# A mixture of experts in full fp32: the order of wide and narrow experts, a narrow expert 0, and ten additions taken off GpSimd

## The chip, the cores and the metric

The kernel runs on one core of one Trainium2 chip. Its time is the device time of one execution, in microseconds (us), here the median of several runs. A profile is one execution recorded instruction by instruction. TensorE, VectorE, ScalarE and GpSimd appear in it as PE (with its weight loads as PEld), DVE, ACT and POOL; SP is the queue that issues the weight loads.

## The reference

A decoder of two layers on 256 tokens of width 1024, all in float32. Layer 0 is retention and a dense SwiGLU; layer 1 is a pooling mixer and a SwiGLU with eight experts, of which each token uses two. Each part starts with an RMSNorm whose output is scaled and shifted by vectors (`mod`) worked out from a second input, and ends in a gated addition to the residual. Cut to what matters here:

```python
h = rmsnorm(x) * (1 + scale) + shift              # scale, shift from c @ ada_w + ada_b
x = x + g1 * pool_mixer(h)                        # window sums, 4 products of 256 x 256, bias, scale
h = rmsnorm(x) * (1 + scale2) + shift2
top, idx = top_k(h @ router, 2); gates = softmax(top)
for e in range(8):                                # each on the tokens that chose it
    y_e = (silu(h_e @ gate[e]) * (h_e @ up[e])) @ down[e]     # 1024 x 3584, 1024 x 3584, 3584 x 1024
x = x + g2 * (sum of a token's two y_e, times its two gates)
return rmsnorm(x)
```

## The kernel before

**Full precision from two rounded halves.** A float32 weight is too exact for TensorE's fast form, so it is taken in two parts. ScalarE writes the rounded weight (`w_hi`), VectorE the remainder (`w_lo = raw - w_hi`), both in `split`, line 109. Weights come through one queue, SP's, as pieces of 128 x 2048 (1.05 MB, "a half": half of the 128 x 4096 that one matrix of one block holds) into a ring of `raw` buffers. Of `w_hi` and `w_lo` there are `N_SPL` = 3 buffers each.

**The expert layer** is 456 to 1371 us of the span. Tokens of an expert are gathered into slots by a product with a one-hot matrix. An expert is worked on in 7 blocks of 512 hidden columns; each block has three matrices (gate, up, down), so six halves. There are 56 blocks, and the program issues for block i: gate, up, and then the down product of block i-2.

- A *wide* expert has 128 slots. Its tokens too are split in a rounded part and a remainder, and each tile takes three matmuls (`mm3`, lines 152 to 154): 24 for a matrix, 72 for a block. TensorE then transposes the product (`moe_T`) and VectorE splits it (`dT<-tbank,dT`).
- A *narrow* expert has 64 slots. Rounded part and remainder of its tokens stand side by side as 128 columns, and two matmuls a tile do the work (`mm2`, lines 731 and 732): 48 for a block. `fold_T` adds the two parts by matmuls with a folding matrix; VectorE has a product (`h_n`) and a split (`dT<-h_n,dT`), each half as long as the wide block's.

The splits of weights, six on ScalarE and six on VectorE, are the same in both kinds.

**The order.** Expert 0 is wide and comes first, while the kernel still works out which experts have more tokens: `ordering()` ranks experts 1 to 7 by their count, the first three are wide, the others narrow. `PLACES` gives the rank worked on at each place: (expert 0), 3, 0, 4, 1, 5, 2, 6. Places 0, 2, 4 and 6 are thus wide and 1, 3, 5 and 7 narrow, each as seven blocks in a row. Around block 5 of an expert `prepare` issues the next one's one-hot matrix, its gather in two or four steps and a transpose; the steps are spread over blocks by `step()`. After an expert's last down product `combine` scales its sum (`take`, VectorE, two halves) and adds it to the residual (`give`, four products). If some expert had more tokens than slots (`room`), a repair pass at the end would work on all experts again.

What sets the order on an engine is the order in which the program issues; what is issued inside `behind(...)` is put after the middle split of the next matrix on its engine. Each engine works through its own list in order and waits on semaphores.

**GpSimd** has 14 instructions. Eight add a column to a column of `mod` in the first stage (line 271, one in each of eight rounds in which VectorE makes two sums for `mod`), two add a 128 x 1024 row to the residual in the pooling mixer (line 505).

Of the kernel before, what the change touches and what calls it, by code (L numbers as in the profile page):

```python
# [10 lines left out]
F = mybir.dt.float32  # L11
# [8 lines left out]
P = 128  # L20
# [25 lines left out]
N_RAW, N_SPL, N_E8 = 6, 3, 4  # L46
# [4 lines left out]
PLACES = (None, 3, 0, 4, 1, 5, 2, 6)  # L51
WIDE = tuple(r is None or r < N_WIDE for r in PLACES)
# [8 lines left out]
def trunk(ctx, tc, x, cols, c_row, const, ada_0, ada, w_0, w_in, w_out, f_gu, f_dn, pool_w, m_g, m_u, m_d, out):  # L61
# [46 lines left out]
    def split(hi, lo, src, engine=nc.vector):  # L108
        return nc.scalar.activation(hi, src, AF.Copy), engine.tensor_sub(lo, src, hi.bitcast(F))  # L109
# [159 lines left out]
    for k in range(KD):  # L269
        ada_sums(ada_0[k], (k, 8 + k), None if k else ada_first)  # L270
        nc.gpsimd.tensor_add(mod[:, k:k + 1], mod[:, k:k + 1], col[:, C_ADAB + k:C_ADAB + k + 1])
# [276 lines left out]
    for b in range(TB):  # L548
# [4 lines left out]
        lT = act.tile([NE, P], F, tag="ohT", name="lT", bufs=2)  # L553
# [12 lines left out]
    above = small([TB, NE, 2, NE], "above")  # L566
# [11 lines left out]
    def sources():  # L578

        def rows(a, i):  # L580
            p, j = divmod(i, NJ)
            if p == 0:
                return a[j * P:(j + 1) * P, :]
            if expert[p] is None:
                expert[p] = nc.values_load(place_i[0:1, PLACES[p]:PLACES[p] + 1], engines=[SP], min_val=1, max_val=NE - 1,
# [50 lines left out]
    def ordering():  # L636
# [9 lines left out]
        over = small([N, 2, N], "over")  # L646
# [6 lines left out]
        at = small([N, N], "at")  # L653
        nc.vector.tensor_tensor(at, rank.rearrange("p (o e) -> p o e", o=1).to_broadcast([P, N, N]),
                                iota[:, 0:N].rearrange("p (r o) -> p r o", o=1).to_broadcast([P, N, N]), op=ALU.is_equal)
        part = small([N, N], "part")
# [17 lines left out]
        nc.vector.memset(room[:, 0:1], float(P))  # L674
# [23 lines left out]
    def prepare(slots, sels, narrow=False, quick=False):  # L698


        oh = one_hot(slots, sels, narrow)
        xe = buf("a8", [KD, 2, HALF] if narrow else [2, KD, P], 2, R, name="xe")
        ohT = buf("ohT", [T], 2, R)
# [3 lines left out]
        def gather(n):  # L707
            ps = tbank()
# [76 lines left out]
    def combine(ye, ohT, gates, g2_row, last=False):  # L785
# [37 lines left out]
    steps = []  # L823

    def step():
        if steps:
            steps.pop(0)()

    def turned_of(i, parts):
        return fold_T(parts) if WIDE[i // NJ] is False else moe_T(parts)  # L830

    def picked(a, placed, p):
        return pick(a, 0) if p == 0 else pick(placed, PLACES[p])

    outs, ths = {}, {}

    def down_of(i):
        p, j = divmod(i, NJ)
# [3 lines left out]
        if j == NJ - 1 and p < NE - 1:  # L842
# [159 lines left out]
```

## Time and profile before

| | |
|---|---|
| time, median of 3 runs | 1397.23 us (1395.9 to 1397.43) |
| the profiled execution: its own time | 1396.38 us |
| its span (first to last instruction) | 1394.1 us |
| granted TensorE clock, mean | 0.994 |
| busy: TensorE, VectorE, ScalarE, GpSimd | 96%, 87%, 70%, 1% |
| weights read | 475 MB, 342 GB/s over the span |

The busy share counts the time in which at least one instruction of the engine was under way. A listed matmul lasts longer than the step from one to the next, since matmuls overlap; their rate is read from starts. A row's "idle before" is the time for which its engine stood still ahead of it, and the name behind `<-` is what ended that.

### The profile page before, as it was taken

To read this page: it belongs to the slowest core of one execution; us is meant where nothing else is said; L and a number is where in the kernel's file an instruction comes from. 1 tells how busy PE (TensorE), PEld (TensorE's weight loads), DVE (VectorE), ACT (ScalarE), POOL (GpSimd) and SP (SyncE) were. 2 spreads that over 40 slices of the span, in tenths; PEclk is the share of its full clock that TensorE was granted. 3 is DMA by queue.
4 is the path that set the end of the run, shared out by engine and by line. 5 is a ranking of instruction groups with operands and counts; after the bars stand their busy time and mean duration, and the time that the engine had idled before them with its cause. 6 is when DMAs were issued, how large, how long until landed. Compare 5 with 4: busy or idle time off the path is not lost.

```text
span 1394.1 us, 16978 instructions
## 1 busy us (share of the span) xinstructions
PE 1336.6 (96%) x6220; PEld 1075.7 (77%) x6220; DVE 1217.7 (87%) x1120; ACT 972.5 (70%) x921; POOL 14.2 (1%) x14
## 2 busy tenths in 40 slices
PE   7999999999998999999999999999999999999996
PEld 5788876888886888877788777878877778887774
DVE  7889867988857898899999799899879989979997
ACT  6555465433435777888877788887778888768885
POOL 1100000000001000000000000000000000000000
PEclk9999999999999999999999999999999999999998
DMA  9977885998786699899999899999989999998980
GB/s 383 373 265 261 323 293 193 356 380 348 272 354 247 252 381 346 314 393 414 393 400 359 329 393 359 421 374 372 379 319 401 398 393 400 358 376 334 386 369 33
DMA packets 66475, 477.32 MB, mean 342 GB/s; under 512 B 7377, under 2 KB 7761, under 8 KB 8658
## 3 DMA queue, kind: packets, MB, share of 16 engines
q1 hardware_dynamic: 66386, 476.17, 88.2%
q8 instruction: 51, 0.84, 0.2%
q14 instruction: 38, 0.31, 0.1%
HBM read 475.10 MB, written 1.05 MB: 342 GB/s over the span
## 4 chain that ended last, share of the span: by engine, by line
PE 67%; DVE 16%; DMA 8%; ACT 4%; issue 4%; SPq 0%; DVEq 0%; ACTq 0%
PE bank L153 18%; PE bank L154 18%; PE bank L152 18%; DVE w_lo L109 13%; DMA raw<-in_m_g_dram 4%; ACT w_hi L109 3%; PE bank L732 3%; PE bank L731 3%; DMA raw<-in_m_u_dram 2%; PE tbank L713 2%; PE tbank L246 1%; PE tbank L767 1%; DMA raw<-in_m_d_dram 1%; DVE xs L804 1%; ACT xe_f L236 1%
## 5 line engine op out<-in xcount | busy, mean ns | idle before, releaser
L109 DVE TENSOR_TENSOR w_lo<-raw,w_hi 128x2048 fp32r<-128x2048 f32 (+1 forms) x413 | 911.9, 2228 | 109.8 <-ACT w_hi L109 108.4
L109 ACT ACTIVATE w_hi<-raw 128x2048 fp32r<-128x2048 f32 (+1 forms) x413 | 765.1, 1866 | 234.1 <-PE bank L154 193.7
L732 PE MATMUL bank<-w_lo,xe 128*128 128x512 f32 x448 | 183.6, 410 | 15.1 <-DVE w_lo L109 11.6
L153 PE MATMUL bank<-w_lo,xe 128*128 128x512 f32 x448 | 176.7, 395 | 6.6 <-DVE w_lo L109 6.2
L731 PE MATMUL bank<-w_hi,xe 128*128 128x512 f32 x448 | 175.7, 393 | 1.4 <-ACT w_hi L109 1.4
L152 PE MATMUL bank<-w_hi,xe 128*128 128x512 f32 x448 | 176.0, 393 | 0.3 <-ACT xe L109 0.3
L154 PE MATMUL bank<-w_hi,xe 128*128 128x512 f32 x448 | 174.6, 390 | 0.0
L152 PE MATMUL bank<-w_hi,T_h 128*128 128x512 f32 x352 | 141.9, 403 | 3.0 <-ACT T_h L109 3.0
L153 PE MATMUL bank<-w_lo,T_h 128*128 128x512 f32 x352 | 140.1, 398 | 2.4 <-DVE w_lo L109 2.4
L154 PE MATMUL bank<-w_hi,T_l 128*128 128x512 f32 x352 | 140.1, 398 | 0.5 <-DVE T_l L109 0.4
L732 PEld LDWEIGHTS bank<-w_lo,xe 128*128 128x128 f32 x448 | 84.1, 188 | 57.4 <-DVE w_lo L109 41.7
L153 PE MATMUL bank<-w_lo,dT 128*128 128x512 f32 x312 | 123.3, 395 | 0.9 <-DVE w_lo L109 0.9
L154 PE MATMUL bank<-w_hi,dT 128*128 128x512 f32 x312 | 121.8, 390 | 0.0
L152 PE MATMUL bank<-w_hi,dT 128*128 128x512 f32 x312 | 114.5, 390 | 0.0
L163 DVE SCALAR_TENSOR_TENSOR raw<-raw,cb 128x1024 f32<-128x1024 f32 x96 | 114.3, 1217 | 0.3 <-DMA raw<-in_ada_dram 0.3
L153 PEld LDWEIGHTS bank<-w_lo,xe 128*128 128x128 f32 x448 | 84.2, 188 | 26.2 <-DVE w_lo L109 9.5
L152 PEld LDWEIGHTS bank<-w_hi,xe 128*128 128x128 f32 x448 | 84.1, 188 | 18.0 <-ACT xe L109 0.5
L731 PEld LDWEIGHTS bank<-w_hi,xe 128*128 128x128 f32 x448 | 84.3, 188 | 17.1 <-ACT w_hi L109 1.8
L154 PEld LDWEIGHTS bank<-w_hi,xe 128*128 128x128 f32 x448 | 84.2, 188 | 17.1
L732 PE MATMUL bank<-w_lo,dT 128*128 128x512 f32 x224 | 82.9, 408 | 2.3 <-DVE w_lo L109 2.2
L152 PEld LDWEIGHTS bank<-w_hi,T_h 128*128 128x128 f32 x352 | 67.2, 191 | 17.6 <-ACT T_h L109 4.0
L153 PEld LDWEIGHTS bank<-w_lo,T_h 128*128 128x128 f32 x352 | 67.5, 192 | 16.8 <-DVE w_lo L109 2.8
(225 smaller groups left out, 1444.1 us busy)
## 6 DMA issues: line engine op xcount, KB each, us to landing
raw<-in_m_g_dram SPq DMA_DIRECT2D x112, 1024.0 KB, 7.2
raw<-in_m_u_dram SPq DMA_DIRECT2D x112, 1024.0 KB, 7.4
raw<-in_m_d_dram SPq DMA_DIRECT2D x112, 1024.0 KB, 7.3
raw<-in_ada_dram SPq DMA_DIRECT2D x48, 1024.0 KB, 7.6
raw<-in_f_gu_dram SPq DMA_DIRECT2D x22, 1024.0 KB, 6.2
raw<-in_w_in_dram SPq DMA_DIRECT2D x16, 1024.0 KB, 4.9
raw<-in_f_dn_dram SPq DMA_DIRECT2D x11, 1024.0 KB, 7.8
raw<-in_w_dram SPq DMA_DIRECT2D x8, 1024.0 KB, 9.1
```

The source lines that it names most:

```text
L109: return nc.scalar.activation(hi, src, AF.Copy), engine.tensor_sub(lo, src, hi.bitcast(F))
L152: nc.tensor.matmul(ps, xh, wh, start=start, stop=False)
L153: nc.tensor.matmul(ps, xh, wl, start=False, stop=False)
L154: nc.tensor.matmul(ps, xl, wh, start=False, stop=stop)
L163: nc.vector.scalar_tensor_tensor(s, s, 1.0, cb, op0=ALU.mult, op1=ALU.mult, accum_out=mod[:, m:m + 1])
L236: nc.scalar.activation(out, ps, AF.Identity, scale=a[:, k:k + 1], bias=s[:, k:k + 1])
L246: nc.tensor.transpose(ps[:, i * P:(i + 1) * P], src[:, i * P:(i + 1) * P], ident)
L713: nc.tensor.matmul(ps[:, i * ns:(i + 1) * ns], xn[:, b, c], oh[:, b, 0:ns], start=(b == 0), stop=(b == TB - 1))
L731: nc.tensor.matmul(ps, x, wh, start=start, stop=False)
L732: nc.tensor.matmul(ps, x, wl, start=False, stop=stop)
L767: nc.tensor.matmul(ps[:, i, c], a[:, c * P:(c + 1) * P], fold, start=True, stop=True)
L804: nc.vector.scalar_tensor_tensor(xs[:, b, c], ps, gates[b], xs[:, b, c], op0=ALU.mult, op1=ALU.add)
```

## The change

1. Expert 0 gets 64 slots instead of 128, so five experts are narrow and three wide.
2. `PLACES` is gone. A list `BLOCKS` gives the expert and the block at each of the 56 steps: the seven blocks of expert 0, and then 49 blocks of which those at t % 7 = 0, 2, 4 belong to the wide experts (places 1 to 3, by rank) and the others to the narrow ones (places 4 to 7). The wide and the narrow experts thus advance side by side, W N W N W N N.
3. For that two experts are prepared in expert 0's blocks 4 and 5, later ones at block 6 of a wide and block 4 of a narrow expert. There is a buffer of its own for narrow experts' gathered tokens (`xe_n`), `ohT` has four buffers instead of two, some small tiles of the ordering share buffers, and the one-hot matrix is issued with the first step of the gather.
4. `combine` takes both halves of the sum at once, and a step is issued after each down product too.
5. GpSimd's eight additions to `mod` become ScalarE activations with a bias; its two additions to the residual go to VectorE.

```diff
-N_RAW, N_SPL, N_E8 = 6, 3, 4
+N_RAW, N_SPL, N_E8, N_OHT = 6, 3, 4, 4
...
-PLACES = (None, 3, 0, 4, 1, 5, 2, 6)
-WIDE = tuple(r is None or r < N_WIDE for r in PLACES)
+WIDE = tuple(0 < p <= N_WIDE for p in range(NE))
+
+_wide = iter([(p, j) for p in range(1, N_WIDE + 1) for j in range(NJ)])
+_narrow = iter([(p, j) for p in range(N_WIDE + 1, NE) for j in range(NJ)])
+BLOCKS = [(0, j) for j in range(NJ)] + [next(_wide if t % 7 in (0, 2, 4) else _narrow) for t in range(7 * NJ)]
...
-        nc.gpsimd.tensor_add(mod[:, k:k + 1], mod[:, k:k + 1], col[:, C_ADAB + k:C_ADAB + k + 1])
+        nc.scalar.activation(mod[:, k:k + 1], mod[:, k:k + 1], AF.Identity, bias=col[:, C_ADAB + k:C_ADAB + k + 1])
...
-        nc.gpsimd.tensor_add(xs[:, b], xs[:, b], gsb_row)
+        nc.vector.tensor_add(xs[:, b], xs[:, b], gsb_row)
...
-        nc.vector.memset(room[:, 0:1], float(P))
+        nc.vector.memset(room[:, 0:1], float(HALF))
...
-        return [lambda: take(0), lambda: (give(0, 0), take(1)), lambda: give(0, 1), lambda: give(1, 0), lambda: give(1, 1)]
+        return [lambda: (take(0), take(1))] + [lambda n=n, b=b: give(n, b) for n in range(2) for b in range(TB)]
...
-    ready = {0: prepare(pick(slot, 0), pick(sel, 0), quick=True)}
+
+    xe_n = buf("a8", [2, KD, 2, HALF], 2, R, name="xe_n")
+    xe_of = lambda p: buf("a8", [2, KD, P], 2, R, name="xe") if WIDE[p] else xe_n[:, (p > 0) * (p + 1) % 2]
+    ready = {0: prepare(xe_of(0), pick(slot, 0), pick(sel, 0), True, True)}
...
     def step():
-        if steps:
-            steps.pop(0)()
+        if first_steps or steps:
+            (first_steps or steps).pop(0)()
...
         if j == NJ - 1 and p < NE - 1:
+            while steps:
+                steps.pop(0)()
             steps.extend(combine(outs[p], ready[p][1], picked(gate, gate_p, p), g2_row))
+            steps.pop(0)()
+
+    def prepare_next(p):
+        ready[p] = prepare(xe_of(p), pick(slot_p, p - 1), pick(sel_p, p - 1), not WIDE[p])
+        first_steps.extend(ready[p][2])
...
-    for i in range(n_blocks):
-        p, j = divmod(i, NJ)
+    for i, (p, j) in enumerate(BLOCKS):
...
             mid = hidden(pg, pu) if wide else (g_out, take_out(pu, "u_out"))
+            if p == 0 and j == 4:
+                prepare_next(1)
+            if p == 0 and j == 5:
+                prepare_next(N_WIDE + 1)
+            if wide and j == NJ - 1 and p < N_WIDE or not wide and j == 4 and N_WIDE < p < NE - 1:
+                prepare_next(p + 1)
             step()
         if i > 1:
             down_of(i - 2)
+            step()
...
-        if j == 5 and p + 1 < NE:
-            ready[p + 1] = prepare(pick(slot_p, PLACES[p + 1]), pick(sel_p, PLACES[p + 1]), not WIDE[p + 1])
-            steps += ready[p + 1][2]
```

VectorE's list before, inside a wide expert (`moe_h` is a wide block's product, `dT<-tbank,dT` the split of its transpose):

```order
L748 TENSOR_TENSOR moe_h<-bank,sg 128x512
L109 TENSOR_TENSOR w_lo<-raw,w_hi 128x2048 x4
L109 TENSOR_TENSOR dT<-tbank,dT 128x512
L109 TENSOR_TENSOR w_lo<-raw,w_hi 128x2048 x2
L748 TENSOR_TENSOR moe_h<-bank,sg 128x512
```

After, at the same place in the list, with a narrow block's product (`h_n`) and split (`dT<-h_n,dT`) between two wide ones:

```order
L755 TENSOR_TENSOR moe_h<-bank,sg 128x512
L113 TENSOR_TENSOR w_lo<-raw,w_hi 128x2048 x4
L113 TENSOR_TENSOR dT<-tbank,dT 128x512
L113 TENSOR_TENSOR w_lo<-raw,w_hi 128x2048 x6
L778 TENSOR_TENSOR h_n<-tbank,sg_n 128x256
L113 TENSOR_TENSOR w_lo<-raw,w_hi 128x2048
L113 TENSOR_TENSOR dT<-h_n,dT 128x4x64
L113 TENSOR_TENSOR w_lo<-raw,w_hi 128x2048
L755 TENSOR_TENSOR moe_h<-bank,sg 128x512
```

The number of splits for a block is six as before; the blocks that they serve now differ in kind from one to the next.

ScalarE's list before, in the first stage's rounds (`hT_f` and `T_h` make the strip of scaled tokens, `w_hi` rounds the next weights):

```order
L109 ACTIVATE w_hi<-raw 128x1024
L265 ACTIVATE xT<-tbank 128x4x128 x2
L236 ACTIVATE hT_f<-xT,mod,a_123 128x256
L109 ACTIVATE T_h<-hT_f 128x256
L109 ACTIVATE w_hi<-raw 128x1024 x2
```

After:

```order
L275 ACTIVATE mod<-mod,col 128x1
L113 ACTIVATE w_hi<-raw 128x1024
L269 ACTIVATE xT<-tbank 128x4x128 x2
L240 ACTIVATE hT_f<-xT,mod,a_123 128x256
L113 ACTIVATE T_h<-hT_f 128x256
L113 ACTIVATE w_hi<-raw 128x1024
L275 ACTIVATE mod<-mod,col 128x1
L113 ACTIVATE w_hi<-raw 128x1024
```

An addition that waits for VectorE's sum now stands ahead of each round's second rounding.

VectorE's list before, in the pooling mixer (`xs` is the residual, `xn_p` the normed tokens):

```order
L226 TENSOR_SCALAR xn_p<-xs,rstd 128x1024
L109 TENSOR_TENSOR w_lo<-raw,w_hi 128x1024 x2
L542 TENSOR_TENSOR xs<-xs,bank 128x512 x2
L234 TENSOR_SCALAR hT_p<-tbank,acol_2738,mod 128x128
```

After:

```order
L230 TENSOR_SCALAR xn_p<-xs,rstd 128x1024
L113 TENSOR_TENSOR w_lo<-raw,w_hi 128x1024
L509 TENSOR_TENSOR xs<-xs,pool_rows 128x1024
L546 TENSOR_TENSOR xs<-xs,bank 128x512 x2
L238 TENSOR_SCALAR hT_p<-tbank,acol_2738,mod 128x128
```

The row's addition (line 509) is now in VectorE's list, ahead of the two additions that need it, and one of two splits has moved behind them.

## Rows read from the trace of the kernel before

**Rows 1.** Busy time, share of the span, and count of each engine.
```profile
span 1394.1 us, 16978 instructions
...
PE 1336.6 (96%) x6220; PEld 1075.7 (77%) x6220; DVE 1217.7 (87%) x1120; ACT 972.5 (70%) x921; POOL 14.2 (1%) x14
```

**Rows 2.** Windows, one for each expert; first row names the columns; PEclk: granted clock.
```profile
core 0: us, PE busy (x) PEld busy (x) DVE busy (x) ACT busy (x) POOL busy (x), PEclk, DMA share, GB/s
456.00:567.80 111.80, 111.77 (x527) 93.03 (x528) 96.67 (x85) 84.03 (x66) 0.00 (x0) 1.00 0.85 318
567.80:674.50 106.70, 102.17 (x508) 83.25 (x506) 101.65 (x64) 92.35 (x81) 0.00 (x0) 1.00 1.00 393
674.50:797.10 122.60, 120.98 (x560) 99.48 (x560) 110.17 (x70) 92.55 (x71) 0.00 (x0) 1.00 0.95 364
797.10:906.50 109.40, 104.81 (x512) 82.85 (x510) 102.06 (x66) 93.28 (x81) 0.00 (x0) 1.00 0.99 391
...
1139.60:1263.70 124.10, 121.38 (x565) 99.88 (x563) 111.32 (x71) 92.66 (x72) 0.00 (x0) 1.00 0.94 359
1263.70:1371.00 107.30, 102.97 (x486) 80.35 (x484) 103.59 (x66) 92.10 (x75) 0.00 (x0) 1.00 0.85 339
sum 915.00, PE 889.50 PEld 720.74 DVE 838.42 ACT 732.52 POOL 0.00; mean PE 111.19 PEld 90.09 DVE 104.80 ACT 91.57 POOL 0.00
```

**Rows 3.** TensorE in time, wide block: start, duration, engine, line, operation, tiles, count.
```profile
518.96 0.60 PE L246 MATMUL tbank<-kp,moe_h 128*128 128x128 f32 x4
...
535.77 0.60 PE L246 MATMUL tbank<-kp,moe_h 128*128 128x128 f32 x4
```

**Rows 4.** VectorE in time, a narrow block.
```profile
1348.43 0.41 DVE L771 TENSOR_TENSOR h_n<-tbank,sg_n 128x256 f32<-128x256 f32 x1
...
1351.34 11.09 DVE L109 TENSOR_TENSOR w_lo<-raw,w_hi 128x2048 fp32r<-128x2048 f32 x5
1362.35 0.42 DVE L771 TENSOR_TENSOR h_n<-tbank,sg_n 128x256 f32<-128x256 f32 x1
```

**Rows 5.** Three engines where wide meets narrow; in brackets idle time before, and releaser.
```profile
1061.76 0.39 PE L154 MATMUL bank<-w_hi,dT 128*128 128x512 f32 x1
...
1061.99 0.39 PE L731 MATMUL bank<-w_hi,xe 128*128 128x512 f32 x1
...
1062.19 3.72 ACT L109 ACTIVATE w_hi<-raw 128x2048 fp32r<-128x2048 f32 x2 [1.75 <-PE bank L154]
...
1064.14 4.49 DVE L109 TENSOR_TENSOR w_lo<-raw,w_hi 128x2048 fp32r<-128x2048 f32 x2 [1.37 <-ACT w_hi L109]
...
1066.49 0.50 PE L732 MATMUL bank<-w_lo,xe 128*128 128x512 f32 x1 [0.48 <-DVE w_lo L109]
```

**Rows 6.** Waits of the load queue: us in total, times, longest.
```profile
SPq L129 <- DVE w_lo L109: 520.4, 237, 7.6
SPq L129 <- DVE dT L109: 52.4, 20, 3.0
```

**Rows 7.** VectorE groups by line and form: busy us, mean ns, idle before.
```profile
L748 DVE TENSOR_TENSOR moe_h<-bank,sg 128x512 f32<-128x512 f32 x28 | 19.1, 683 | 0.0
```

**Rows 8.** VectorE and GpSimd in time, in the pooling mixer.
```profile
426.74 4.52 DVE L109 TENSOR_TENSOR w_lo<-raw,w_hi 128x1024 fp32r<-128x1024 f32 x2
426.96 3.22 POOL L505 TENSOR_TENSOR xs<-xs,pool_rows 128x1024 f32<-128x1024 f32 x1 [4.05 <-ACT w_hi L109]
...
431.19 1.27 DVE L542 TENSOR_TENSOR xs<-xs,bank 128x512 f32<-128x512 f32 x2
```

**Rows 9.** The last of the first stage's eight rounds, in time.
```profile
54.15 0.08 DVE L163 DVE_READ_ACCUMULATOR raw<-raw,cb 128x1 f32 x1
...
54.31 1.10 POOL L271 TENSOR_TENSOR mod<-mod,col 128x1 f32<-128x1 f32 x1 [4.79 <-DVE raw L163]
...
55.55 1.22 DVE L109 TENSOR_TENSOR w_lo<-raw,w_hi 128x1024 fp32r<-128x1024 f32 x1
...
56.68 1.04 ACT L109 ACTIVATE w_hi<-raw 128x1024 fp32r<-128x1024 f32 x1
```

More of the change, by code (lines that the diff above doesn't have):

```diff
@@ L106, in trunk, with split @@
         nc.vector.tensor_copy(cb[:, 512 * h:512 * (h + 1)], ps)
-    def split(hi, lo, src, engine=nc.vector):
-        return nc.scalar.activation(hi, src, AF.Copy), engine.tensor_sub(lo, src, hi.bitcast(F))
+    def split(hi, lo, src):
+        return nc.scalar.activation(hi, src, AF.Copy), nc.vector.tensor_sub(lo, src, hi.bitcast(F))
     @contextmanager
@@ L552, in trunk @@
             nc.tensor.matmul(ps[0:NE, 0:P], rt[:, k], xT[b][:, k], start=(k == 0), stop=(k == KD - 1))
-        lT = act.tile([NE, P], F, tag="ohT", name="lT", bufs=2)
+        lT = act.tile([NE, P], F, tag="ohT", name="lT", bufs=N_OHT)
         nc.scalar.activation(lT, ps[0:NE, 0:P], AF.Copy)
@@ L565, in trunk @@
     lg_e = lg.rearrange("p b (e o) -> p b e o", o=1).to_broadcast([P, TB, NE, NE])
-    above = small([TB, NE, 2, NE], "above")
+    above = buf("oh", [TB, NE, 2, NE], name="above")
     gt, eq = above[:, :, :, 0], above[:, :, :, 1]
@@ L580, in rows @@
         def rows(a, i):
-            p, j = divmod(i, NJ)
+            p, j = BLOCKS[i]
             if p == 0:
@@ L584, in rows @@
             if expert[p] is None:
-                expert[p] = nc.values_load(place_i[0:1, PLACES[p]:PLACES[p] + 1], engines=[SP], min_val=1, max_val=NE - 1,
+                expert[p] = nc.values_load(place_i[0:1, p - 1:p], engines=[SP], min_val=1, max_val=NE - 1,
                                            skip_runtime_bounds_check_because="a permutation of 1 to 7")
@@ L645, in ordering @@
         ce = cnt[:, 1:].rearrange("p (e o) -> p e o", o=1).to_broadcast([P, N, N])
-        over = small([N, 2, N], "over")
+        tmp = buf("oh", [4 * N * N], name="tmp")
+        over = tmp[:, 0:2 * N * N].rearrange("p (e i j) -> p e i j", e=N, i=2)
         nc.vector.tensor_tensor(over[:, :, 1], cj, ce, op=ALU.is_equal)
@@ L652, in ordering @@
         nc.vector.tensor_reduce(rank, over.rearrange("p e i j -> p e (i j)"), axis=AX.X, op=ALU.add)
-        at = small([N, N], "at")
+        at = tmp[:, 2 * N * N:3 * N * N].rearrange("p (r e) -> p r e", r=N)
         nc.vector.tensor_tensor(at, rank.rearrange("p (o e) -> p o e", o=1).to_broadcast([P, N, N]),
                                 iota[:, 0:N].rearrange("p (r o) -> p r o", o=1).to_broadcast([P, N, N]), op=ALU.is_equal)
-        part = small([N, N], "part")
+        part = tmp[:, 3 * N * N:].rearrange("p (r e) -> p r e", r=N)
         def take(a, out):
@@ L696, in one_hot, with prepare @@
         return oh
[L698 to L703, printed above, removed]
+    def prepare(xe, slots, sels, narrow=False, quick=False):
+        oh = None
+        ohT = buf("ohT", [T], N_OHT, R)
         ns = HALF if narrow else P
@@ L707, in gather @@
         def gather(n):
+            nonlocal oh
+            if n == 0:
+                oh = one_hot(slots, sels, narrow)
             ps = tbank()
@@ L907, in trunk @@
             nc.vector.tensor_copy(sl, sel[:, :, ds(e, 1)])
-            xe, ohT, steps = prepare([se[:, b] for b in range(TB)], [sl[:, b] for b in range(TB)])
+            xe, ohT, steps = prepare(buf("a8", [2, KD, P], 2, R, name="xe"), [se[:, b] for b in range(TB)],
+                                     [sl[:, b] for b in range(TB)])
             for step in steps:
```

10 lines of the change are left out of this document (5 added, 5 removed).

## The prediction, made before the changed kernel was run

> **What bounds the kernel now.** I read the totals first: the span is 1394.1 us and every engine but GpSimd looks loaded, TensorE 96%, VectorE 87%, ScalarE 70% [rows 1]. TensorE's share says little, because a matmul's listed 0.39 us overlaps the next one, which starts 0.23 us later [rows 5]. So I cut the expert layer into its eight experts by the first matmul of each and asked for busy time per stretch [rows 2]. The layer runs from 456 to 1371 us, two thirds of the span, at a granted clock of 1.00. The reader is to see two kinds of stretch. Experts 2, 4 and 6 in the order of work are wide and take 122.6 to 124.1 us each with VectorE 90% busy; experts 1, 3, 5 and 7 are narrow and take 106.7 to 109.4 us with VectorE 93 to 97% busy. Over the layer VectorE is busy 838.4 of 915 us: 77 us is all that a perfect order could give.
>
> Third, single blocks. An undisturbed wide block takes 16.81 us, from one block's transposes to the next [rows 3]: 72 matmuls at 0.23 us and four transposes, TensorE without a gap. An undisturbed narrow block takes 13.92 us [rows 4]: from one small product to the next, 1348.43 to 1362.35: six splits at 2.20 us (five take 11.01 to the start of the next operation) and two small operations, 0.7 us together, VectorE without a gap. Fourth, the weights: the load queue waits almost only for VectorE to give a buffer back [rows 6], so the transfers follow and do not lead; at 393 GB/s [rows 2] the 1.05 MB of a half matrix take 2.7 us, and the prefetch buffers even that out.
>
> Fifth, the waits where a wide and a narrow block meet [rows 5]. TensorE ends its last wide matmul at 1061.99; ScalarE, which had waited 1.75 us for that buffer, starts its rounding at 1062.19; VectorE, idle 1.37 us, starts the remainder at 1064.14; TensorE, idle 0.48 us, uses it at 1066.49. So a weight buffer given back is usable 4.5 us later, and there are three. This loop decides the case.
>
> **The change part by part.** Expert 0 in 64 slots. Seven blocks go from 72 to 48 matmuls each, and the first stretch is no longer TensorE's. VectorE's work in it was 96.7 us [rows 2]. A narrow block has 0.70 us of small operations where a wide one has two of 0.60 (listed 683 ns, with 0.08 under the next one [rows 7]): 7 x 0.5 = 3.5 less. The stretch now prepares two experts, not one: about 1.7 more. That leaves 94.9; at the 93.3% of a narrow stretch (102.06 of 109.4) it is 101.7 us against 111.8: 10 us saved. The ordering arithmetic, which lay under TensorE's matmuls, is now on VectorE's path and is in the 94.9.
>
> Wide and narrow in turn. In 49 blocks nothing is added or removed; 21 wide and 28 narrow ones stand in the order W N W N W N N. The hope in it is that VectorE works ahead in a wide block and spends the lead in the next narrow one. How far can it work ahead? Three wide halves take TensorE 3 x 2.74 = 8.2 us (12 matmuls each); the loop needs 4.5 + 2.74 = 7.2. The lead is 1.0 us, no more, whatever the order. Worked half by half from these three durations (TensorE takes a half when it is ready; a half is ready 2.20 after the last one, plus small operations, or 4.5 after the half three places earlier was finished, whichever is later): a wide block starts at 0.4 and keeps TensorE until 16.7; the six halves of the narrow one are ready at 15.9, 18.5, 21.2, 23.4, 26.2 and 28.4, and the next wide half at 30.6. A pair takes about 30.3 to 30.6 us; apart they take 16.81 + 13.92 = 30.7. The narrow block's foldings (1.6 us of TensorE) fall into its own waits. So alternation by itself gives next to nothing: 0 to 2 us over 21 pairs, and I take 0.
> What each expert needs besides, its gather and its combination, costs in either kind of stretch: a narrow expert is 109.4 - 7 x 13.9 = 12 us over its blocks, a wide one 122.6 to 124.1 - 7 x 16.8 = 5 to 6.5, since a wide stretch hides part of VectorE's share under TensorE. One of six such preparations has moved into expert 0's stretch: 4 us saved here (its cost is in the 10 above). How much of the rest a mixed order hides the trace does not show. Bounds: at worst all pay as in a narrow stretch, 3 x 6 = 18 us more; at best all pay as in a wide one, 4 x 6 = 24 less. I take 4 us less, near the middle, since three of seven blocks are wide.
>
> Three buffers hold nothing else up: the two experts' sums hold four banks, which leaves two for gate and up, and each is read within the 5.5 us in which TensorE does the down matmuls of another block; both halves of a combination are now taken at once, so the banks come back before the next expert asks.
>
> GpSimd's additions. The eight small ones go to ScalarE, ahead of the rounding of the next strip, so that rounding now waits for VectorE's sum, and VectorE's remainder waits behind it. In the last of the eight rounds the sum ends at 54.23, an addition of 0.2 and a rounding of 1.04 end at about 55.6, and VectorE wants the strip at 55.55 [rows 9]: 0 to 0.15 us a round, together 0 to 1 us lost. GpSimd's own 1.10 us lay beside VectorE's second sum, so nothing comes back. The two long ones go to VectorE, about 1.2 us each (as two halves of 512, 1.27 [rows 8]). While GpSimd's second one ran, 426.96 to 430.18, two splits of VectorE took 4.52 us [rows 8] where one alone takes 1.22 [rows 9]: 2 us come back there, and 1.2 + about 0.7 for the first are paid. Net of all ten: between 1 lost and 1 saved; I take 0.
>
> Sum: -10 - 4 - 4 = -18 us. The profiled execution takes 1396.38 us, 2.3 more than its span; the median shown is 1397.23. I forecast 1379.
>
> The Perfetto Trace Analysis page of the Trainium skill (Optimization Strategy) advises, where the most-contended engine changes from stretch to stretch, to interleave the stretches; by it the 77 us of VectorE's idle time would be what this change is after. The same section says that a gap which repeats can mean too few buffers for the next tile; rows 5 show just that gap, and by that sentence interleaving without more buffers gives little. The trace agrees with the second; only the run can tell on the first.
>
> **The rivals.** (1) Mixing pays: gathers and combinations vanish into the block kind that has room, and VectorE stays busy as in the last narrow stretch, 103.59 of 107.3 or 96.5%. Its 838 us, less 3 or 4, then take 866 where they took 915: 49 saved, 1348; without any gap, 1319. For it: no stretch shows that VectorE must wait as long as TensorE lags. Against it: the lead of 1.0 us. This is what the page's interleaving rule would make of the case. (2) Slower: each border between kinds costs both engines, as in rows 5: VectorE 1.37 and TensorE 0.48 us. There are 21 wide blocks with a narrow one behind, where before seven blocks had such borders (three switches to narrow with two affected blocks, and the last): 14 more x 1.85 = 26 us, and combinations that then fall on both engines as at the worst bound, 18: 1397 - 14 + 44 = 1427 in full, about 1406 with half of it. It decides once a border's cost, net, passes 0.7 us. Against it: the half-by-half count, which contains the loop, finds no loss. (3) No change: expert 0's gain is paid back by the extras of the mixed part, +14 against -14: 1397. (4) That the change sets off the repair pass: were any expert over its room, all eight would be worked on again, some 900 us. The reference's router gives 49 tokens to expert 0 and 40, 68, 81, 50, 59, 62 and 103 to the others on these inputs; the three over 64 get 128 slots. Excluded.
>
> **How the numbers follow.** Forecast (1379, own range 1367 to 1392): 0.50. Rival 1: 0.22. Rival 2: 0.14. Rival 3: 0.14. A difference of 0.2%, 2.8 us, is about what can be told from no change here. Faster by more: nearly all of the forecast (0.48), all of rival 1 (0.22), a third of rival 3 (0.05): 0.75. Within: 0.11. Slower: 0.14. The range reaches down through the larger part of rival 1, to 1346, and up to 1402, where rival 2 begins; about one in ten is left out on either side.
>
> **What would show it.** Right: expert 0's seven blocks take about 102 us; W and N in turn take 30 to 32 us a pair where nothing is prepared, with TensorE idle before narrow halves and ScalarE still waiting for buffers in wide ones; VectorE is busy 93 to 94% of the layer; the splits beside 428 us are back at 1.2 us. Wrong: pairs of 29 us or VectorE at 96% and over (rival 1); pairs over 32 us, with both engines idle at each border (rival 2); a first stretch that takes as long as before, or a wait of the load queue for anything but its buffers.

## The result, and the profile after

The changed kernel takes 1375.19 us (median of four runs, 1374.0 to 1376.74) against 1396.78 for the one before: a ratio of 0.9846, 95% interval 0.9829 to 0.9864. The forecast was 1379, a gain of 18; the gain is 21.6. The profiled execution took 1376.74 us with a span of 1375.0, so between the two profiles there are 19.1 us of span to be explained.

First the totals of the profile after (beside them [rows 1]). VectorE's and TensorE's shares are as they were in a shorter span; GpSimd is left with 0.2 us.

```profile
span 1375.0 us, 16794 instructions
...
PE 1315.1 (96%) x6136; PEld 1052.5 (77%) x6136; DVE 1215.2 (88%) x1121; ACT 978.2 (71%) x942; POOL 0.2 (0%) x4
```

Then the expert layer, cut in both kernels at the first weight matmul of the layer, of the eighth block and of the last block (columns as in [rows 2]). Before:

```profile
456.03:567.77 111.74, 111.74 (x526) 93.00 (x527) 96.62 (x85) 84.00 (x66) 0.00 (x0) 1.00 0.85 318
567.77:1355.43 787.66, 762.43 (x3613) 616.01 (x3612) 726.51 (x458) 634.61 (x517) 0.00 (x0) 1.00 0.97 379
1355.43:1394.10 38.67, 26.10 (x105) 17.37 (x103) 29.41 (x30) 21.80 (x26) 0.00 (x0) 0.90 0.09 33
```

After:

```profile
458.88:556.93 98.05, 93.85 (x475) 76.16 (x476) 88.38 (x76) 85.83 (x85) 0.00 (x0) 0.98 0.88 347
556.93:1330.95 774.02, 754.40 (x3554) 605.31 (x3552) 726.13 (x450) 633.61 (x506) 0.00 (x0) 1.00 0.98 388
1330.95:1375.00 44.05, 29.67 (x121) 20.41 (x119) 34.34 (x38) 23.23 (x28) 0.00 (x0) 0.91 0.07 26
```

The stretch of expert 0 is 13.7 us shorter. The 48 blocks after it are 13.6 shorter: VectorE is busy for the same 726 us and idle for 47.9 instead of 61.1. The end is 5.4 longer, since the last wide expert's combination now falls into it. And the layer starts 2.85 us later (458.88 against 456.03). -13.7 - 13.6 + 5.4 + 2.85 = -19.1.

That late start hides two opposite things. Up to the router's products the changed kernel is 4.85 us ahead (the first transpose of `xs` behind the last pooled addition stands at 437.45 instead of 442.30); the first gather then loses 7.7. Only 3.2 us of that lead lie in the pooling mixer, between the second token half's norm (`xn_p`) and the gather's first matmul (451.16 - 426.07 = 25.09 before, 446.29 - 424.43 = 21.86 after). The other 1.64 are there already ahead of it, and they are not the change's: narrow0, below, whose program is the same as before's up to the gather, is 2.6 ahead at that point. Before:

```profile
426.07 0.76 DVE L226 TENSOR_SCALAR xn_p<-xs,rstd 128x1024 f32<-128x1024 f32 x1
...
451.16 3.81 PE L713 MATMUL tbank<-oh,xn_m 128*128 128x128 f32 x32 [0.74 <-DVE oh L695]
...
456.03 0.50 PE L152 MATMUL bank<-w_hi,xe 128*128 128x512 f32 x1 [0.26 <-ACT xe L109]
```

VectorE and TensorE in time, after:

```profile
424.43 0.75 DVE L230 TENSOR_SCALAR xn_p<-xs,rstd 128x1024 f32<-128x1024 f32 x1
...
446.29 0.41 PE L720 MATMUL tbank<-oh,xn_m 128*128 128x64 f32 x2 [0.74 <-DVE oh L696]
...
446.65 4.83 PE L720 MATMUL tbank<-oh,xn_m 128*128 128x64 f32 x30
...
452.25 1.12 PE L187 MATMUL tbank<-kp,mod 128*128 128x128 f32 x4 [0.56 <-ACT ohT L732]
454.06 1.11 PE L187 MATMUL tbank<-kp,mod 128*128 128x128 f32 x4 [0.69 <-ACT g_row L193]
455.86 1.02 PE L645 MATMUL tbank<-sel,one 128*128 128x8 f32 x4 [0.69 <-ACT g_row L193]
458.88 0.80 PE L738 MATMUL bank<-w_hi,xe_n 128*128 128x512 f32 x1 [2.01 <-DVE xe_n L113]
```

From the first gather matmul to the first weight matmul it takes 12.6 us (451.16 to 456.03, 4.9, before). Three things are to be seen: the gather is one run of 32 matmuls for all eight tiles; the gate row (L187, L193), which the program issues after block 0's first products, stands ahead of them in TensorE's list (so the order of issue alone, as told ahead of the prediction, does not settle the order); and a weight matmul takes 0.43 us from start to start at first where it takes 0.23 later. ScalarE's part, after, with the gate row's copies among the evictions:

```profile
451.52 0.40 ACT L240 ACTIVATE xe_f<-tbank,mod,acol 128x64 f32<-128x64 f32 x1 [6.79 <-PE tbank L720]
...
453.40 0.60 ACT L193 ACTIVATE g_row<-tbank 128x512 f32<-128x512 f32 x1 [0.67 <-PE tbank L187]
...
455.20 0.60 ACT L193 ACTIVATE g_row<-tbank 128x512 f32<-128x512 f32 x1 [0.91 <-PE tbank L187]
455.70 0.40 ACT L240 ACTIVATE xe_f<-tbank,mod,acol 128x64 f32<-128x64 f32 x1
457.37 0.63 ACT L113 ACTIVATE xe_n<-xe_f 128x512 fp32r<-128x512 f32 x1 [1.27 <-DVE xe_f L238]
```

The granted clock is the third from last column in stretches of 5 us; it falls to 0.50, the lower of its two levels (1.2 of 2.4 GHz), where before it stayed at 1.00 in this stretch. Before:

```profile
450.00:455.00 5.00, 4.22 (x36) 3.97 (x35) 1.91 (x9) 0.92 (x2) 0.00 (x0) 1.00 0.98 413
455.00:460.00 5.00, 4.40 (x19) 3.50 (x20) 2.41 (x5) 2.69 (x6) 0.00 (x0) 1.00 0.05 20
```

After:

```profile
445.00:450.00 5.00, 4.26 (x33) 4.20 (x33) 1.37 (x7) 0.00 (x0) 0.00 (x0) 0.85 1.02 429
450.00:455.00 5.00, 3.76 (x16) 2.83 (x16) 1.03 (x3) 1.97 (x5) 0.00 (x0) 0.50 0.38 162
455.00:460.00 5.00, 2.31 (x8) 1.85 (x8) 3.02 (x19) 1.52 (x3) 0.00 (x0) 0.50 0.00 0
460.00:465.00 5.00, 5.00 (x19) 4.02 (x18) 2.70 (x12) 2.72 (x2) 0.00 (x0) 0.79 0.01 3
```

In the mixed part, a wide and a narrow block with nothing prepared, after:

```profile
1270.45:1300.72 30.27, 30.27 (x141) 24.47 (x140) 28.88 (x17) 25.38 (x19) 0.00 (x0) 1.00 1.01 424
```

30.27 us a pair was forecast as 30.3 to 30.6. TensorE is listed busy without a gap, and its count comes to about 29.3 us: 120 weight matmuls at 0.23, some 27.3 us, and about 2 of foldings and transposes. VectorE is busy 28.9. Over the whole mixed part the pairs take 28.7 to 37.4 us, since gathers and combinations fall on some of them.

In the pooling mixer the two splits beside which GpSimd ran ([rows 8], 4.52 us) are back at what one alone takes. VectorE, after:

```profile
425.10 1.22 DVE L113 TENSOR_TENSOR w_lo<-raw,w_hi 128x1024 fp32r<-128x1024 f32 x1
426.24 1.22 DVE L509 TENSOR_TENSOR xs<-xs,pool_rows 128x1024 f32<-128x1024 f32 x1
427.37 1.40 DVE L546 TENSOR_TENSOR xs<-xs,bank 128x512 f32<-128x512 f32 x2
...
429.01 1.22 DVE L113 TENSOR_TENSOR w_lo<-raw,w_hi 128x1024 fp32r<-128x1024 f32 x1
```

### The profile page after: what moved, and what is told of

It reads as the page before. It is cut to its first block, busy times and chain, and to the rows that moved or that the text cites. A ratio compares the mean times of both kernels' runs of the same rounds, so it can differ in the third digit from the quotient of the medians.

```text
span 1375.0 us, 16794 instructions
## 1 busy us (share of the span) xinstructions
PE 1315.1 (96%) x6136; PEld 1052.5 (77%) x6136; DVE 1215.2 (88%) x1121; ACT 978.2 (71%) x942; POOL 0.2 (0%) x4
## 4 chain that ended last, share of the span: by engine, by line
PE 70%; DVE 16%; ACT 6%; issue 4%; DMA 3%; DVEq 0%; SPq 0%; ACTq 0%
PE bank L157 15%; PE bank L158 15%; PE bank L156 14%; DVE w_lo L113 12%; PE bank L739 8%; PE bank L738 7%; PE tbank L774 3%; ACT w_hi L113 3%; DMA raw<-in_m_d_dram 2%; PE tbank L720 2%; PE tbank L250 1%; DVE raw L167 1%; ACT xe_f L240 1%; DMA raw<-in_m_u_dram 1%; DVE dT L113 1%
## 5 line engine op out<-in xcount | busy, mean ns | idle before, releaser
L739 PE MATMUL bank<-w_lo,xe_n 128*128 128x512 f32 x560 | 230.7, 412 | 12.7 <-DVE w_lo L113 9.6
L738 PE MATMUL bank<-w_hi,xe_n 128*128 128x512 f32 x560 | 221.1, 396 | 2.0 <-DVE xe_n L113 2.0
L739 PEld LDWEIGHTS bank<-w_lo,xe_n 128*128 128x128 f32 x560 | 105.8, 189 | 57.5 <-DVE w_lo L113 38.0
L157 PE MATMUL bank<-w_lo,xe 128*128 128x512 f32 x336 | 132.5, 394 | 0.9 <-DVE w_lo L113 0.9
L156 PE MATMUL bank<-w_hi,xe 128*128 128x512 f32 x336 | 131.6, 392 | 0.0
L158 PE MATMUL bank<-w_hi,xe 128*128 128x512 f32 x336 | 130.9, 390 | 0.0
L738 PEld LDWEIGHTS bank<-w_hi,xe_n 128*128 128x128 f32 x560 | 106.0, 189 | 22.1 <-DVE xe_n L113 2.1
L738 PE MATMUL bank<-w_hi,dT 128*128 128x512 f32 x280 | 100.1, 394 | 1.7 <-DVE dT L113 1.7
L158 PE MATMUL bank<-w_hi,dT 128*128 128x512 f32 x256 | 99.8, 390 | 0.0
L156 PE MATMUL bank<-w_hi,dT 128*128 128x512 f32 x256 | 94.2, 389 | 0.0
L158 PEld LDWEIGHTS bank<-w_hi,T_l 128*128 128x128 f32 x352 | 66.5, 189 | 17.1 <-DVE T_l L113 3.2
L157 PEld LDWEIGHTS bank<-w_lo,xe 128*128 128x128 f32 x336 | 63.1, 188 | 16.3 <-DVE w_lo L113 3.8
```

Source lines behind the costliest of these rows:

```text
L156: nc.tensor.matmul(ps, xh, wh, start=start, stop=False)
L157: nc.tensor.matmul(ps, xh, wl, start=False, stop=False)
L158: nc.tensor.matmul(ps, xl, wh, start=False, stop=stop)
L738: nc.tensor.matmul(ps, x, wh, start=start, stop=False)
L739: nc.tensor.matmul(ps, x, wl, start=False, stop=stop)
```

## The experiments

Layer times below run from the layer's first weight matmul to the end of the span: 938.1 us before, 916.1 after. They leave out what precedes the layer. The kernel before took 1396.91, 1396.09 and 1396.70 us beside the first, second and third four, so times of different groups can be set against each other to about 1 us.

### First four: one part alone, or one part undone

**narrow0**: the kernel before with expert 0 narrow.

```diff
-WIDE = tuple(r is None or r < N_WIDE for r in PLACES)
+WIDE = tuple(r is not None and r < N_WIDE for r in PLACES)
...
-        nc.vector.memset(room[:, 0:1], float(P))
+        nc.vector.memset(room[:, 0:1], float(HALF))
...
-    ready = {0: prepare(pick(slot, 0), pick(sel, 0), quick=True)}
+    ready = {0: prepare(pick(slot, 0), pick(sel, 0), True, True)}
```

> The kernel before with one part of the change: expert 0 in 64 slots, its room set to 64; order of experts, combination and GpSimd's additions as before. Theory: expert 0's stretch goes from 111.7 to about 97 us (98.05 in the changed kernel, which prepares two experts in it and not one), but starts some 7 us later, since in the changed kernel the first gather of a narrow expert took 12.6 us from its first matmul to the first weight matmul where the wide one took 4.9 before; together about 1397 - 14 + 7 = 1390 us. Rival: the late start comes from something else in the changed kernel (its moved additions, its clock), and here the stretch starts at 456 us as before: 1383 us or less.

1388.13 us (ratio 0.9933, 0.9916 to 0.9949). The profile is of the longest of its four runs, 1391.65. In it the first weight matmul came at 461.89, 5.9 late, expert 0's stretch took 94.5, the layer 927.7. The loss in the first gather belongs to the narrow gather, not to the moved additions.

**whole**: the changed kernel, experts one after the other.

```diff
-BLOCKS = [(0, j) for j in range(NJ)] + [next(_wide if t % 7 in (0, 2, 4) else _narrow) for t in range(7 * NJ)]
+ORDER = (0, 1, 4, 2, 5, 3, 6, 7)
+BLOCKS = [(p, j) for p in ORDER for j in range(NJ)]
...
-            if p == 0 and j == 4:
-                prepare_next(1)
...
+            if j == 4 and p != ORDER[-1]:
+                prepare_next(ORDER[ORDER.index(p) + 1])
```

> The changed kernel with one part undone: the experts are worked on whole, one after the other, in the order 0, 1, 4, 2, 5, 3, 6, 7 (narrow, wide, narrow, wide, ...), each next one prepared in block 4. Theory of the prediction: taking turns block by block is worth 0 to 2 us in itself and about 4 for hidden gathers and combinations, so this is 2 to 8 us slower than the changed kernel: 1377 to 1383 us. Rival: the waits between the engines, gone through half by half with three buffers, give 109.9 us for seven blocks in whole experts and 107.7 in turns; seven times 2.2 is 16 us: about 1390 us.

1381.25 us (0.9879, 0.9858 to 0.99), layer 919.7: taking turns is worth 3.6 us in the layer and 6 in the times (single runs of whole spread from 1377.29 to 1382.06). The rival's 16 is out.

**gps_back**: the changed kernel with GpSimd's additions.

```diff
-        nc.scalar.activation(mod[:, k:k + 1], mod[:, k:k + 1], AF.Identity, bias=col[:, C_ADAB + k:C_ADAB + k + 1])
+        nc.gpsimd.tensor_add(mod[:, k:k + 1], mod[:, k:k + 1], col[:, C_ADAB + k:C_ADAB + k + 1])
...
-        nc.vector.tensor_add(xs[:, b], xs[:, b], gsb_row)
+        nc.gpsimd.tensor_add(xs[:, b], xs[:, b], gsb_row)
```

> The changed kernel with all ten additions back on GpSimd. Theory: they held up the work before the expert layer by the 4.9 us by which the changed kernel's router is earlier; the lead comes about 1 us in the first stage's rounds, 1 more around 70 us, 2.5 in the pooling mixer: 1380 us, and the router's products at 442 us again. Theory of the prediction: their price is nothing, 1374 to 1376 us.

1377.63 us (0.9867, 0.9848 to 0.9885): 2.4 more than the changed kernel, but the intervals overlap; neither theory is met. At 72 us it is 3.0 ahead of the kernel before, the changed kernel 2.0, so the eight small additions are not what was gained there. It is the clock: narrow0 is 3.0 ahead too, with the same program as before up to there, and from 65 to 70 us the granted clock was 0.54 before, 0.66 after, and 1.00 in narrow0 and gps_back. The two long additions do cost: its gather comes 2.65 us later than the changed kernel's, 25.14 us after the second `xn_p` instead of 21.86.

This run also parts the 7.7 us of the first gather. Its gather is the changed kernel's, one run for eight tiles with the gate row ahead of the first weights, but the clock stays at 1.00 until 457 us:

```profile
448.94 0.41 PE L720 MATMUL tbank<-oh,xn_m 128*128 128x64 f32 x2 [0.74 <-DVE oh L696]
...
458.83 0.79 PE L738 MATMUL bank<-w_hi,xe_n 128*128 128x512 f32 x1 [2.01 <-DVE xe_n L113]
```

```profile
450.00:455.00 5.00, 3.66 (x31) 3.23 (x31) 0.69 (x2) 1.86 (x5) 0.00 (x0) 1.00 0.47 198
455.00:460.00 5.00, 2.31 (x11) 1.78 (x12) 3.42 (x21) 1.64 (x4) 0.00 (x0) 0.71 0.01 3
```

From the first gather matmul to the first weight matmul that is 9.9 us, where before took 4.9 and the changed kernel, at half the clock, 12.6: some 5.0 for the longer chain and 2.7 for the clock. early_wide, whose clock fell only at 453.6, has 9.9 as well.

**early_wide**: the last wide block one place earlier.

```diff
-next(_wide if t % 7 in (0, 2, 4) else _narrow)
+next(_wide if t % 7 in ((0, 2, 3) if t >= 42 else (0, 2, 4)) else _narrow)
```

> The changed kernel with the last wide block four places from the end and not three (the last seven blocks are W N W W N N N), so that the last wide expert's combination ends before the last weights are used up. Theory: the end after the last block's start, 44.1 us in the changed kernel and 38.7 before, gets 5 us shorter, and the blocks before get up to 3 longer, since VectorE is their limit: 1371 to 1374 us. Rival: VectorE has the same work and no idle time to put it in: no change, 1375.

1377.25 us (0.9859, 0.9843 to 0.9876): no gain, a miss. The end still takes 44.5 us and the 48 blocks take 776.0 instead of 774.0. The combination did move forward, but VectorE has no idle time there to put it in. VectorE's idle time in the end is 9 to 11 us in all three kernels (before, after, early_wide), so the 5.4 us are its work, which another order can only move: two_grouped, below, ends in 38.7 us and has longer blocks.

### Second four: the first gather, and the buffers

**gating_late**: gate row and ordering held back on ScalarE and VectorE.

```diff
-            gate, g2_row = gating()
+            with behind_next():
+                gate, g2_row = gating()
```

> The changed kernel with the gates' softmax, the gate row and the ordering held on ScalarE and VectorE until after the middle split of the next weights. In the changed kernel ScalarE's two copies of the gate row stand between the four evictions of the first expert's gathered tokens (451.5 to 456.1 us). Theory A (these copies are the late start): the first weight matmul comes 2 to 3 us earlier, 1372 to 1373 us. Theory B (TensorE's clock, 0.50 there, is the late start): no earlier than by 1 us, 1375.

1377.46 us (0.9866, 0.9849 to 0.9882). Theory A's start came true, 455.39 instead of 458.88, and nothing was left of it: the clock fell a little later, TensorE's first two blocks took 21.8 us where they had taken 18.8, and expert 0's stretch 101.95. The clock is not shown to be the whole cause: gps_back had it at 0.50 for 5.1 us of that stretch, nearly as long as here (6.2), and took 98.7. Here the ordering's arithmetic, which the changed kernel does while VectorE waits for the first weights (from 457.3 on), also comes between the remainders (from 468.4 on).

```profile
450.00:455.00 5.00, 2.09 (x16) 1.42 (x14) 1.74 (x5) 2.52 (x6) 0.00 (x0) 0.97 0.48 202
455.00:460.00 5.00, 4.61 (x11) 3.65 (x12) 0.33 (x1) 1.22 (x1) 0.00 (x0) 0.50 0.01 3
460.00:465.00 5.00, 5.00 (x21) 3.92 (x20) 3.36 (x2) 3.70 (x4) 0.00 (x0) 0.84 0.20 29
```

**two_steps**: the first gather in two steps of four tiles.

```diff
-        per = 512 // ns
+        per = 4 if quick else 512 // ns
...
-                split(xe[:, :, 0], xe[:, :, 1], t)
+                split(xe[:, per * n:per * (n + 1), 0], xe[:, per * n:per * (n + 1), 1], t)
```

> The changed kernel with the first expert's gather in two steps of four tiles (64 columns each), as the wide gather had it, and not one of eight. Theory C (one step of eight tiles makes the first weight matmul wait for all eight evictions): the first weight matmul comes 4 to 6 us earlier, 1369 to 1371 us. Theory B (the clock): 1 to 2 us earlier, 1373 to 1374.

1369.46 us (0.9812, 0.9795 to 0.9828), the fastest kernel of this study. The first weight matmul comes at 451.56, 7.3 earlier, 5.0 us after the first gather matmul; the gate row's broadcast is no longer ahead of it, and the clock stays up (the last row is expert 0's stretch):

```profile
445.00:450.00 5.00, 4.26 (x39) 4.19 (x38) 1.71 (x8) 0.81 (x2) 0.00 (x0) 1.00 1.01 428
450.00:455.00 5.00, 4.18 (x20) 3.23 (x20) 1.84 (x5) 3.33 (x6) 0.00 (x0) 1.00 0.40 164
455.00:460.00 5.00, 5.00 (x28) 3.99 (x26) 4.57 (x3) 5.00 (x5) 0.00 (x0) 1.00 0.24 48
...
451.60:549.60 98.00, 94.00 (x487) 75.97 (x488) 88.87 (x84) 87.58 (x89) 0.00 (x0) 1.00 0.90 349
```

**wide_gather**: the same, with 128 columns a matmul, half of them unread.

```diff
-        per = 512 // ns
+        per, ng = (4, P) if quick else (512 // ns, ns)
...
-                    nc.tensor.matmul(ps[:, i * ns:(i + 1) * ns], xn[:, b, c], oh[:, b, 0:ns], start=(b == 0), stop=(b == TB - 1))
+                    nc.tensor.matmul(ps[:, i * ng:(i + 1) * ng], xn[:, b, c], oh[:, b, 0:ng], start=(b == 0), stop=(b == TB - 1))
...
-                split(xe[:, :, 0], xe[:, :, 1], t)
+                split(xe[:, per * n:per * (n + 1), 0], xe[:, per * n:per * (n + 1), 1], t)
```

> The changed kernel with the first gather as before: two steps of four tiles, 128 columns each, of which 64 are read. It gives TensorE twice the columns in the gather. Theory B (64 columns a matmul are what the clock falls on): the granted clock stays 1.00 from 445 to 460 us and the first weight matmul comes at 451 us, about 4.9 us after the first gather matmul: 1367 to 1369 us. Theory C: the same as two_steps, at whatever clock.

1370.04 us (0.9816, 0.9799 to 0.9832), first weight matmul at 451.58, clock 1.00. The same as two_steps, so the columns are not the point: 64 at a time kept the clock too. Theory C holds, whose forecast this is.

**spl4_raw4**: four buffers of rounded weights and remainders.

```diff
-N_RAW, N_SPL, N_E8, N_OHT = 6, 3, 4, 4
+N_RAW, N_SPL, N_E8, N_OHT = 4, 4, 4, 4
```

> The changed kernel with four buffers of rounded weights and remainders, not three, and four raw buffers in the ring, not six (the memory of both is the same). Theory of the prediction (three buffers limit the lead of VectorE over TensorE to 1.0 us): the lead is 3.7 us; half by half seven blocks in turns take 101 us and not 107.7, so up to 45 us less, 1330 us or somewhat more, with ScalarE's wait for TensorE's buffers (58.8 us on the wide blocks' matmuls) mostly gone. Rival: the loads are the limit by now (DMA share 0.98 in the part in turns): with two raw buffers less it is the same or slower, 1375 to 1400, and ScalarE waits for DMA instead.

1371.91 us (0.9824, 0.9807 to 0.984). The 48 blocks took 772.4 us instead of 774.0, and most pairs took the same to a few hundredths: the model of three buffers that limit the lead is wrong for this part. ScalarE's wait for the wide blocks' buffers fell as it should, 58.8 to 23.3 us, and other waits on TensorE took its place. ScalarE's waits, after:

```profile
ACT w_hi L113 <- PE bank L158: 58.8, 68, 3.1
ACT w_hi L113 <- PE bank L738: 13.0, 28, 0.9
```

With four buffers:

```profile
ACT g_out L766 <- PE bank L739: 45.7, 23, 3.5
ACT dT L113 <- DVE h_n L778: 28.7, 18, 2.3
ACT w_hi L113 <- PE bank L158: 23.3, 34, 2.1
```

Nor are the loads the limit, for all their DMA share of 0.98: of ScalarE's waits 14.1 us in 770 are put down to loads after, and none with four buffers. Added up in the order in which packets land, each half is in memory at least 17 us before ScalarE rounds it in the mixed part after, and at least 10 with four raw buffers. What limits a pair is in the row shown above: by its count TensorE has about 1 us of room in 30.27.

### Third four: each part again, from the two-step gather

**two_narrow0**: narrow0 with the gather of two_steps (both diffs above).

> The kernel before with expert 0 in 64 slots and, so that the clock doesn't fall, its gather in two steps of four tiles (in narrow0 it was one step of eight, the granted clock was 0.50 from 450 to 465 us and the first weight matmul came at 461.9). Theory: what the gather cost there comes back: the stretch of expert 0 starts at 455 to 456 us and takes 96 to 98, 1382 to 1384 us, and the price of one part alone (expert 0 narrow) is some 13 us gained. Rival: the clock falls all the same, and it stays at 1388.

1384.98 us (0.9913, 0.9898 to 0.9927); two of its six runs took 1380.93 and 1381.69, at a mean granted clock of 0.993, the others 1384.87 to 1386.47, at 0.988. So the same program was some 4 us slower where the clock was lower; at which point it fell in those runs no profile shows. The profile is of the run of 1381.69: first weight matmul at 455.32, clock 1.00 there, expert 0's stretch 93.6, layer 924.1. In the layer the clock was 0.50 for 3.4 us twice, each time behind a wait of 2.4 us of TensorE where a wide expert follows a narrow one (658.0 and 893.5), so up to 3.4 us of the 924.1 are the clock's.

**two_whole**: two_steps with the experts whole (as in whole).

> two_steps (the changed kernel with the first gather in two steps, 1369.5 us) with the experts worked on whole, as in the run whole. Theory: taking turns is worth what the layer lost in whole's profile, 3.6 us from the first weight matmul on, up to the 6 that the times showed: 1373 to 1375.5. Rival: whole and the changed kernel differ by the clock in their first gathers alone: 1369 to 1370.

1374.13 us (0.9834, 0.982 to 0.9847), layer 919.6. Turns are worth 4.0 us in the layer (915.5 in two_steps) and 4.7 in the times, with no fall of the clock from the router to the last down product in either profile. Expert 0's stretch and the blocks after it, without turns:

```profile
452.40:544.40 92.00, 89.32 (x448) 71.69 (x449) 86.61 (x80) 84.31 (x79) 0.00 (x0) 1.00 0.91 359
544.42:1333.15 788.73, 765.64 (x3608) 611.51 (x3606) 731.81 (x462) 638.23 (x518) 0.00 (x0) 1.00 0.97 382
```

In two_steps, with turns:

```profile
549.60:1323.80 774.20, 754.42 (x3553) 605.25 (x3552) 726.06 (x450) 633.55 (x505) 0.00 (x0) 1.00 0.97 388
```

So the 4.0 are a difference: the 48 blocks are 14.5 us shorter with turns, but expert 0's stretch, in which two experts are prepared and not one, is 6.0 longer, and the end 4.5.

**two_grouped**: two_steps, three wide blocks and then four narrow ones.

```diff
-t % 7 in (0, 2, 4)
+t % 7 in (0, 1, 2)
```

> two_steps with the mixed blocks in the order W W W N N N N, not W N W N W N N: the experts still advance side by side, but three wide and four narrow blocks stand together. Theory of the prediction's lead (VectorE can be 1 us ahead, so only neighbours even each other out): most of what turns are worth goes, 1372 to 1374 us. Rival (what counts is that gathers and combinations of one kind fall on blocks of the other, in whatever order): 1369 to 1370.

1374.71 us (0.9838, 0.9824 to 0.9852), layer 919.5: as without turns. Its 48 blocks take 782.8 us, 5.9 less than without turns, and the preparation in expert 0's stretch costs as much. Neighbours even each other out; groups of three and four are already too long for most of it.

**two_gps**: two_steps with GpSimd's additions (as in gps_back).

> two_steps with the ten additions back on GpSimd, at a clock that does not fall in the gather. Theory: the router is 2 to 2.5 us later by the pooling mixer's two long additions, and nothing is lost in the first stage: 1371.5 to 1372 us, the first weight matmul at 453.5 to 454. Theory of the prediction: no difference, 1369 to 1370.

1376.41 us (0.9851, 0.9837 to 0.9865): 7.0 us dearer than two_steps, more than either theory. From the second `xn_p` to the first gather matmul it takes 25.09 us, two_steps 21.90: 3.2 for the long additions. The five profiles with GpSimd's additions have 25.09 to 25.14, the eight with VectorE's (spl4_raw4, whose buffers differ, left out) 21.86 to 21.90. The first weight matmul came 3.8 later (455.36), expert 0's stretch and the end took 1.6 and 2.2 more. The clock fell in this kernel though its gather has two steps, and once more in the end (0.83 from 1350 to 1360 us):

```profile
445.00:450.00 5.00, 3.90 (x26) 3.14 (x23) 2.68 (x14) 1.76 (x3) 0.00 (x0) 1.00 1.00 413
450.00:455.00 5.00, 4.52 (x32) 4.12 (x30) 1.39 (x6) 1.56 (x5) 0.00 (x0) 0.72 0.67 280
455.00:460.00 5.00, 4.64 (x13) 3.70 (x14) 1.07 (x3) 2.30 (x4) 0.00 (x0) 0.60 0.01 3
```

## Why the prediction was right, and where its steps failed

That the time was right to 4 us is in part luck, because errors of opposite sign met. The layer got 22.0 us shorter (938.1 to 916.1) where the sum had 18, and the pooling mixer 3.2 where it had 0; the first gather lost 7.7 that were not in the sum; and 1.64 of the 19.1 between the two profiles lie ahead of the pooling mixer, where profiles of one program differ by as much: -22.0 - 3.2 - 1.6 + 7.7 = -19.1. In layer time, steps of the profiles: 938.1 before, 924.1 with expert 0 narrow (two_narrow0), 919.6 with the new steps of preparation and combination (two_whole), 915.5 with turns (two_steps; 916.1 after).

- *Expert 0 in 64 slots, -10.* Measured -13.7 in its stretch, in which two experts are prepared, and -13.9 in the layer of two_narrow0, from which two falls of the clock take up to 3.4 away. The mechanism is right; the term that was mis-sized is VectorE's work in the stretch, 94.9 us forecast and 88.4 measured. The 96.7 of the first stretch of before [rows 2] was taken as if a stretch held all of one expert's work; it held 37 remainders of weights where the new one holds 36, and part of the ordering's arithmetic, which the sum puts into the new stretch, ran before it began. The 1.7 for a second preparation did not come on top either: both stretches hold three splits of gathered tokens and four one-hot operations. What preparing a second expert there costs is waiting more than work: 6.0 us of stretch for 2.3 of VectorE (two_steps against two_whole).
- *Extras hidden better, -4, a preparation moved, -4, and turns, 0 (0 to 2).* The first two come with the mixed order, so two_steps against two_whole holds all three: 4.0 us in the layer, 4.7 in the times, half of the 8. No run separates them. The other 4.5 us, from two_narrow0 to two_whole, are the new steps of preparation and combination, which the sum did not have as a term, and the clock's up to 3.4 told above; how much of them the steps are stays open.
- *The reason given for turns.* The pair of 30.27 us is as forecast, but the reason given for it, "This loop decides the case", fell: with a fourth buffer the pairs take the same time. What did survive is the consequence that neighbouring blocks even out and groups hardly do, by two_grouped, without the loop as its cause. By its count TensorE sets the pair: I set its 96% aside because listed matmuls overlap. That objection holds for the listed durations; the count of matmuls times the 0.23 us from start to start would have shown a nearly full TensorE, 29.3 of 30.27 us.
- *GpSimd's additions, 0 (-1 to +1).* Wrong for the two long ones: they cost 3.2 us on the way to the gather. The two splits beside them are back at 1.22 us each, as forecast; that the long additions stood on the way to the router was not seen. The eight small ones cost nothing either way: the changed kernel leads the one before by 0.80 us at 20 us and by 0.79 at 75. That two_gps was 7.0 dearer in all is not shown to be theirs: the other 3.8 lie where the clock fell, and before and two_narrow0, with the same additions on GpSimd, have profiles in which it did not fall between router and experts.
- *Missing: the first gather.* The prediction lets expert 0's stretch begin where it did. A narrow gather fills one bank with eight tiles, so the first weight matmul waits for all of them, the gate row slips in, and the clock falls: +7.7 us, some 5.0 for the chain and 2.7 for the clock (gps_back), against which the two steps give 7.3 back. It is in the code of `prepare` (`per = 512 // ns`), and should have been read there: "64 slots" changes the gather's steps, not only the matmuls.
- *The end, +5.4.* Also not foreseen; by early_wide and two_grouped it is work that has to be done somewhere.

Rival 1 (1348) asked for VectorE at 96.5%; it is at 93.8% (726.13 of 774.02) in the mixed part. TensorE's listed share there is 97.5%; by count and step an estimate gives about 94% (2806 listed weight matmuls and 48 of the combinations at 0.23 us, 698 others at 0.11), so neither engine is full over the whole part, and what keeps both from more outside undisturbed pairs stays open. By the Trainium skill's page Perfetto Trace Analysis (Optimization Strategy), a kernel whose most-contended engine changes over time may gain by interleaving such stretches; two_whole against two_steps agrees in sign, at 4.7 us of the 77 at stake. The same section of the Trainium skill's page says that a gap which repeats, on the engine that should be saturated, can mean too few buffers; the gap of rows 5 did not mean that, as the fourth buffer gave 1.6 us in 774. Rival 2 (slower borders) is out, since the pairs lose nothing; rival 4 as well. Some readings were off without consequence: 1061.99 in rows 5 is the start of the next matmul (the last wide one is listed to 1062.15), an addition on ScalarE took 0.29 us and not 0.2, and half of rival 2 adds up to 1405.

Left open: why the clock falls. It fell in the changed kernel during the gather, in early_wide, with the same instructions up to there, only after it (0.86, then 0.50), and in two_gps but not in two_steps. No run set it on purpose: the 5.0 and 2.7 us rest on profiles in which it happened to fall at different moments.

## What to carry to other kernels

Before saying which engine bounds a stretch, count each engine's work at its start-to-start rate: in an undisturbed pair that gave 97% for TensorE beside VectorE's 95%, and the order of work was worth 4 us of 920, however long the idle times looked side by side. When a size changes, read every helper that derives a step count from it; here a smaller expert turned a gather of two steps into one and delayed everything behind it. A gain in one part can be lost just behind it, as gating_late's 3.5 us were, so look at the next stretch too, and at the granted clock in short stretches around each place where TensorE waits. And set two profiles side by side from a common event: the lead of 4.85 us held 1.64 that the same program also shows against itself.

## What the runs showed of the hardware that was not expected

The granted clock fell to 0.50 for 6.8 to 17.1 us between router and experts (448 to 467 us), in the profiles of eight kernels (after, narrow0, whole, gps_back, early_wide, gating_late, spl4_raw4, two_gps) and not in those of the other six; the weight matmuls then took 0.43 us from start to start instead of 0.23. In five of them (after, narrow0, whole, spl4_raw4, two_gps) it fell while TensorE was still at the gather, in the others behind it. All seven kernels with the one-step gather had the fall, and one of the seven with two steps (two_gps), so the shorter chain goes with a steady clock but does not ensure it. A GpSimd addition of 128 x 1024 took 3.22 us beside VectorE's splits and nearly doubled the time of these, 4.52 us for two ([rows 8]) that take 1.22 each without it; on VectorE the addition takes 1.22.
